# Second layer of a bidirectional recurrent trunk: gate groups in four parts between the projection units, the square root of 1 - a a in another form, and the convolution's first tap on ScalarE

## The chip, the core and the metric

The kernel runs on one core of a Trainium2 chip. A core has a matrix engine (TensorE, PE in the rows; its weight loads are a queue of their own, PEld), VectorE (DVE), ScalarE (ACT), GpSimd (POOL) and SyncE (SP), which issues the DMAs. Each engine works through its own instructions in order and waits for the others on semaphores. The metric is the device time of one launch in microseconds; a comparison of this kernel tells a change of about 1% from no change.

## What is computed

The reference is one step of a two-layer trunk with width D = 1024 on T = 1152 tokens, 128 of context and 1024 latents. Layer 0 (a gated recurrence and an attention) isn't touched by the change. Layer 1, cut to what matters:

```python
def odd_mixer(h, w_in, w_out, conv_w, conv_b, gate_w, gate_b, lam, s0):
    xb, g = jnp.split(h @ w_in, 2, axis=-1)
    xc = centred_dwconv(xb, conv_w, conv_b).astype(jnp.float32)   # width 4
    ...
    for d in range(2):
        gates = jnp.einsum('bthi,ghij->gbthj', xblk, gate_w[d].astype(jnp.float32)).reshape(2, B, T, W_C)
        gates = gates + gate_b[d].astype(jnp.float32)[:, None, None, :]
        r = jax.nn.sigmoid(gates[0])
        i = jax.nn.sigmoid(gates[1])
        log_a = -RG_C * r * jax.nn.softplus(-lam[d].astype(jnp.float32))
        a = jnp.exp(log_a)
        u = jnp.sqrt(-jnp.expm1(2.0 * log_a)) * (i * xc)
        ...
        hs, h_fin = linear_recurrence(a, u, s0[:, d].astype(jnp.float32))
    y = ((outs[0] + outs[1]) * jax.nn.silu(g.astype(jnp.float32))).astype(h.dtype)
    return y @ w_out, jnp.stack(finals, axis=1)
```

The gate matrices are block diagonal: 8 blocks of 128 features, two directions d, two gates each.

## The kernel before, in words

Features lie on the partitions, tokens along the free axis, in 3 chunks of 384. Every product is made of three matmuls, since operands are split into a high and a low part (names ending in h and l). In layer 1 the input projection is a sequence of 48 units (a block of 128 features times a chunk), of 24 matmuls each (L316 to L318). Its order, `ORD1`, is the x branch of blocks 0 to 3, then the g branch of block 0, x of block 4, g of block 1 and so on, and g of blocks 4 to 7 at the end. An x unit is copied by ScalarE to `xp`; a g unit is turned by ScalarE and VectorE (L1161) into `sg`.

Around the units stands the work of each block j, at positions in the sequence that the tables `PF`, `PC`, `PK`, `PS` and `PY` give (block by block; the change leaves them as they are):

- `conv` at `PC`: four taps on VectorE (L1049 makes `xc` from `xp`, L1051 three more), then the split into `xch` and `xcl` for the matmuls.
- `gates` at `PF`: for each direction and chunk, a group of 3 matmuls for each of two gates, 12 groups a block. The groups of the r gate go to the PSUM tag a (`ps_a`), those of the i gate to the tag b (`ps_b`), two banks each. ScalarE takes each group out by a tanh (`gr` from `ps_a`; `yT` or `gi` from `ps_b`).
- `rg_exp`, right behind the gates: on ScalarE `rt` = tanh of the decay's exponent and `gr` = a by exp; then `ra` = a a (GpSimd at L1102 for d = 0, ScalarE for d = 1) and on VectorE (1 + a a) times `rt` (L1103).
- `rg_sqrt` at `PS`: two square roots on ScalarE, which need a table of their own: an ACT_TABLE_LOAD stands ahead of them, and one behind them for the next tanh.
- `rg_scan` at `PK`: the input of the recurrence (L1116 on VectorE, L1118 on GpSimd, which multiplies by `rt`), seven scans on VectorE (L1127) and the sum of both directions (L1132). `y_fin` (L1167) multiplies by `sg`.

A unit's product lies in a PSUM bank of the tag mm (three banks) or, every fourth unit, of the tag o (one bank). A unit can't start before the bank that it takes over has been read, by the copy to `xp` or by L1161.

The order on each engine isn't written out: a scheduler takes the operations in the order in which the program writes them as their priority, and lays down one queue for each engine. What the tables say is therefore where an operation is written, and the queues follow from that and from the scheduler's own view of when operands are there. The output projection behind the units (L984 to L986) accumulates over 8 blocks k; its first two tiles take the terms of blocks 6 and 7 last.

Of the kernel before, what the change touches and what calls it, by code (L numbers as in the profile page):

```python
# [1 line left out]

# [16 lines left out]
CW = 384  # L19
# [3 lines left out]
# columns of the packed small parameters (feature on the partition)  # L23
# [10 lines left out]
def trunk_kernel(ctx: ExitStack, tc: tile.TileContext, x, wm0, wm, bmr, wfe, wv, woe, wfo, woo, rgw, sm, st0,  # L34
# [34 lines left out]
    def act(out, in_, func, **kw):  # L69
        """An activation; those that need a table of their own stay between its load and the next one."""  # L70
# [12 lines left out]
    # ------------------------------------------------------------------ constants  # L83
# [39 lines left out]
    # decay floors: the first entry of the softmax over the two logits  # L123
# [12 lines left out]
    # log1p(exp(-|lam|)) + max(-lam, 0), as a series in z = e / (2 + e) <= 1/3  # L136
# [17 lines left out]
    V.tensor_scalar(rgc, sp_t[3], 4.0, None, OP.mult)  # L154
# [3 lines left out]
    # ------------------------------------------------------------------ weight stream  # L158
# [43 lines left out]
    # ------------------------------------------------------------------ adaLN rows  # L202
# [86 lines left out]
    def to_hT2(l, c, ks, xn, tag):  # L289
        """Two blocks at once, each engine's steps together."""  # L290
# [18 lines left out]
    # ------------------------------------------------------------------ units of the projections  # L309
# [10 lines left out]
    def unit_f(i, c, tag=None):  # L320
        """Features of one block of 128 on the partition, one chunk of tokens."""
# [7 lines left out]
    def unit_v(i, t):  # L329
        """Tokens on the partition, 256 features."""  # L330
# [29 lines left out]
    def gate_evac(key, o, twice=False):  # L360
        """o sigmoid(o); twice that by way of sigmoid(o) = (1 + tanh(o / 2)) / 2."""
# [22 lines left out]
    # ------------------------------------------------------------------ start  # L384
# [81 lines left out]
    # ------------------------------------------------------------------ layer 0, gated recurrence  # L466
# [17 lines left out]
    def ew1(h, d):  # L484
        """Log decays, their running sums in chunks of 64 and the sums' distances from each chunk's middle."""
# [877 lines left out]
```

## Time and profile before

| | us |
|---|---|
| median of three runs | 1321.14 (1316.18 to 1326.65) |
| span of the profiled execution | 1308.3 |
| time of the profiled execution itself | not recorded apart from its span |
| median less span | 12.8 |
| granted TensorE clock over the span (1 is full) | 0.972 |
| TensorE busy over the span | 1210.3 (93%) |
| stretch of layer 1 that the rows look at, from the span's start | 925 to 1210 |

The span is the time between the first and the last instruction of one execution on the chip. In the rows, L-numbers are lines of the kernel before, `out<-in` the names of the tiles, an amount in brackets behind `<-` the idle time of the engine ahead of the instruction and what ended it. "x24" is a number of instructions. Where a group's row has two numbers behind the bar, the first is its whole time and the second the mean of one in ns.

### The profile page before, as it was taken

How to read it: one execution, taken by the hardware profiler on the slowest of the kernel's cores; microseconds unless marked ns; L12 is line 12 of the kernel's file. 1: busy time of each engine (PE TensorE's matmuls, PEld its weight loads, DVE VectorE, ACT ScalarE, POOL GpSimd, SP SyncE). 2: the span in 40 equal slices, each digit the busy share in tenths (PEclk: the TensorE clock that was granted, in tenths of full speed). 3: DMA queues.
4: the chain of work that ended last, by engine and by line, in shares of the span. 5: the costliest groups of instructions: out<-in, count | busy, mean ns of one | idle time of the engine just before them, and what ended most of it. 6: DMA issues, size and time to landing. Idle time of an engine off the chain costs nothing.

```text
span 1308.3 us, 19176 instructions
## 1 busy us (share of the span) xinstructions
PE 1210.3 (93%) x7536; PEld 1076.2 (82%) x7536; DVE 692.2 (53%) x1422; ACT 540.4 (41%) x1065; POOL 380.4 (29%) x271
## 2 busy tenths in 40 slices
PE   4999999999999966999989999999989898988998
PEld 3889998999998964779966667888989798987886
DVE  5547128316365100000058897555568978799844
ACT  3435134334253201111136675323376676777311
POOL 0143023321414101111150420025445663645000
PEclk8999999999999997999979999999999989999999
DMA  9401000111101236562240215324001101112432
GB/s 353 179 33 37 17 19 23 53 33 37 33 23 43 95 120 208 173 209 75 65 158 13 95 66 177 113 81 145 17 25 41 41 25 41 41 33 81 145 129 81
DMA packets 41909, 110.45 MB, mean 84 GB/s; under 512 B 4180, under 2 KB 14804, under 8 KB 41820
## 3 DMA queue, kind: packets, MB, share of 16 engines
q1 hardware_dynamic: 41820, 109.24, 24.4%
q8 instruction: 59, 0.97, 0.3%
q14 instruction: 30, 0.25, 0.1%
HBM read 96.61 MB, written 12.61 MB: 83 GB/s over the span
## 4 chain that ended last, share of the span: by engine, by line
PE 36%; DVE 12%; ACT 6%; issue 4%; POOL 2%; DMA 1%; POOLq 0%; ACTq 0%; DVEq 0%; SPq 0%
PE ps_mm L316 5%; PE ps_mm L318 5%; PE ps_mm L317 5%; PE ps_mm L985 5%; PE ps_mm L984 4%; PE ps_mm L986 4%; DVE yT L1127 2%; DVE xc L1051 2%; DVE P L849 2%; ACT P L77 2%; ACT gr L77 1%; PE ps_a L221 1%; DMA bmrow<-in_bmr_dram 1%; DVE ps_mm L844 1%; ACT rt L77 1%
## 5 line engine op out<-in xcount | busy, mean ns | idle before, releaser
L316 PE MATMUL ps_mm<-hTh,wh 128*128 128x384 f32 x936 | 320.7, 347 | 9.9 <-ACT xp L77 4.8
L317 PE MATMUL ps_mm<-hTl,wh 128*128 128x384 f32 x936 | 319.8, 342 | 2.3 <-DVE hTl L307 1.7
L318 PE MATMUL ps_mm<-hTh,wl 128*128 128x384 f32 x936 | 319.4, 341 | 0.7 <-POOL wl L186 0.7
L186 POOL TENSOR_TENSOR wl<-wraw,wh 128x1024 fp32r<-128x1024 f32 x50 | 127.2, 2548 | 306.1 <-ACT wh L77 248.7
L316 PEld LDWEIGHTS ps_mm<-hTh,wh 128*128 128x128 f32 x936 | 177.8, 191 | 26.5 <-issue 6.5
L317 PEld LDWEIGHTS ps_mm<-hTl,wh 128*128 128x128 f32 x936 | 178.4, 191 | 4.8 <-DVE hTl L307 3.3
L318 PEld LDWEIGHTS ps_mm<-hTh,wl 128*128 128x128 f32 x936 | 178.2, 190 | 1.3 <-POOL wl L186 1.0
L985 PE MATMUL ps_mm<-wl,yh 128*128 128x512 f32 (+1 forms) x288 | 113.4, 394 | 4.6 <-DVE wl L186 4.5
L984 PE MATMUL ps_mm<-wh,yh 128*128 128x512 f32 (+1 forms) x288 | 112.7, 393 | 0.0
L986 PE MATMUL ps_mm<-wh,yl 128*128 128x512 f32 (+1 forms) x288 | 112.3, 390 | 0.0
L77 ACT ACTIVATE wh<-wraw 128x1024 fp32r<-128x1024 f32 x68 | 71.3, 1057 | 91.1 <-DMA wraw<-in_wfe_dram 67.3
L262 POOL TENSOR_TENSOR ss<-ss,nhalf 128x1 f32<-128x1 f32 x27 | 15.3, 565 | 242.9 <-DVE ss L261 185.8
L339 PE MATMUL ps_mm<-wh,hTh 128*128 128x256 f32 x288 | 82.6, 287 | 2.4 <-ACT va L77 2.4
L341 PE MATMUL ps_mm<-wh,hTl 128*128 128x256 f32 x288 | 81.2, 282 | 0.0
L340 PE MATMUL ps_mm<-wl,hTh 128*128 128x256 f32 x288 | 81.0, 281 | 0.0
L365 DVE SCALAR_TENSOR_TENSOR yT<-yT,ps_mm 128x384 f32<-128x384 f32 x10 | 5.5, 554 | 131.3 <-ACT yT L77 131.3
L77 ACT ACTIVATE res<-xt 128x512 f32<-128x512 f32 (+1 forms) x37 | 22.9, 619 | 123.3 <-DVE xt L994 115.5
L814 POOL TENSOR_TENSOR nbm<-mkt,bT 128x384 f32<-128x384 f32 x42 | 45.5, 1108 | 90.1 <-DVE nm L860 40.4
L985 PEld LDWEIGHTS ps_mm<-wl,yh 128*128 128x128 f32 x288 | 54.6, 189 | 19.0 <-DVE wl L186 7.7
L984 PEld LDWEIGHTS ps_mm<-wh,yh 128*128 128x128 f32 x288 | 54.5, 189 | 12.4 <-issue 0.3
L986 PEld LDWEIGHTS ps_mm<-wh,yl 128*128 128x128 f32 x288 | 54.4, 189 | 11.4
L1118 POOL TENSOR_TENSOR yT<-yT,rt 128x384 f32<-128x384 f32 x42 | 56.4, 1370 | 23.4 <-ACT rt L77 19.4
(260 smaller groups left out, 2477.3 us busy)
## 6 DMA issues: line engine op xcount, KB each, us to landing
wm<-in_wm_dram SPq DMA_DIRECT2D x48, 512.0 KB
wraw<-in_wfe_dram SPq DMA_DIRECT2D x28, 512.0 KB
xt<-in_x_dram SPq DMA_DIRECT2D x18, 512.0 KB
bT<-in_bias_dram SPq DMA_DIRECT2D x48, 192.0 KB
wraw<-in_wfo_dram SPq DMA_DIRECT2D x16, 512.0 KB
x_d<-xt SPq DMA_DIRECT2D x9, 512.0 KB
xt<-x_d SPq DMA_DIRECT2D x9, 512.0 KB
out_dram<-xt SPq DMA_DIRECT2D x18, 256.0 KB
```

The source lines that it names most:

```text
L77: i = A.activation(out, in_, func, **kw)
L186: (lo_eng or G).tensor_tensor(lo, r, hi.bitcast(F32), OP.subtract)
L316: PE.matmul(o, w1, hh, start=(k == 0), stop=False)
L317: PE.matmul(o, w1, hl, start=False, stop=False)
L318: PE.matmul(o, w2, hh, start=False, stop=(k == 7))
L339: PE.matmul(o, hh, w1, start=(k == 0), stop=False)
L340: PE.matmul(o, hh, w2, start=False, stop=False)
L341: PE.matmul(o, hl, w1, start=False, stop=(k == 7))
L984: PE.matmul(o[:, :q - p], yh[:, z], wh[:, p:q], start=(k == 0), stop=False)
L985: PE.matmul(o[:, :q - p], yh[:, z], wl[:, p:q], start=False, stop=False)
L986: PE.matmul(o[:, :q - p], yl[:, z], wh[:, p:q], start=False, stop=(k == 7))
L1118: G.tensor_tensor(us[c], us[c], r[:, c * CW:(c + 1) * CW], OP.mult)
```

## The change

Three edits, all in layer 1.

The first splits the gates. Before, `rg_front(j)` wrote all 12 groups of a block and both `rg_exp` at position `PF[j]`. Now `gates(j, part)` writes three groups at a time, at the positions `PF[j]` + 0, 1, 2 and 3 (no later than `PS[j]`), with a unit between; the groups alternate between `ps_a` and `ps_b`. `rg_exp(j, 0)` follows part 1, `rg_exp(j, 1)` part 3.

The second computes the square root of 1 - a a as (1 + a) times the square root of tanh(y / 2), with y the negative logarithm of a. The tanh's factor `rgc` is halved, `ra` and L1103 go, and after each square root VectorE multiplies by (1 + a) (line 1111 of the kernel after).

The third makes the convolution's first tap an activation (Identity with a scale and a bias for each partition) on ScalarE.

```diff
-    V.tensor_scalar(rgc, sp_t[3], 4.0, None, OP.mult)
+    V.tensor_scalar(rgc, sp_t[3], 2.0, None, OP.mult)
...
-        V.tensor_scalar(acc, xp[:, 0:1155], w[0], smc("convb", j), OP.mult, OP.add)
+        act(acc, xp[:, 0:1155], AF.Identity, scale=w[0], bias=smc("convb", j))
...
-    def gates(j, d):
+    GD = {}
+    GROUPS = [(d, c, q) for d in range(2) for c in range(3) for q in range(2)]
+
+    def gates(j, part):
...
+        for d, c, q in GROUPS[3 * part:3 * part + 3]:
...
+        if part == 1:
+            GD.pop((j, 0))
+            rg_exp(j, 0)
+        if part == 3:
+            GD.pop((j, 1))
             XS.pop(j)
             gw.pop(j)
+            rg_exp(j, 1)
...
         act(t, r, AF.Tanh, scale=rgc[:, ci], bias=rgc[:, ci])
         act(r, r, AF.Exp, scale=nrgc[:, ci], bias=nrgc[:, ci])
-        t2 = slab("ra")
-        if d:
-            act(t2, r, AF.Square)
-        else:
-            G.tensor_tensor(t2, r, r, OP.mult)
-        V.scalar_tensor_tensor(t, t2, 1.0, t, op0=OP.add, op1=OP.mult)
 
     def rg_sqrt(j, d):
         act(RT[j, d], RT[j, d], AF.Sqrt, scale=0.25)
+        V.scalar_tensor_tensor(RT[j, d], GR[j, d], 1.0, RT[j, d], op0=OP.add, op1=OP.mult)
...
-        for p, f in ((max(ends[j], PC[j]), conv_all), (PF[j], rg_front), (PS[j], rg_root), (max(PK[j], PS[j]), rg_back),
+        for p, f in ((max(ends[j], PC[j]), conv_all), *[(min(PF[j] + n, PS[j]), partial(gates, part=n)) for n in range(4)],
+                     (PS[j], rg_root), (max(PK[j], PS[j]), rg_back),
```

The numbers of instructions: TensorE's matmuls and the 26 table loads are the same; GpSimd loses 8 `ra`; ScalarE loses 8 squares and gains 8 first taps; VectorE loses 8 first taps, and 16 products with (1 + a a) become 16 with (1 + a).

Three places show how the queues move. The first is ScalarE around the first square roots of layer 1, those of block 0. Before, all six r gates of block 0 (`gr` from `ps_a`) and both exp stand there, then the square roots of `rt`; the five `yT` behind them are the i gates of the next block, whose r gates come later:

```order
L77 ACTIVATE gr<-ps_a,hgb 128x384 x4
L77 ACTIVATE rt<-gr,rgc 128x1152
L77 ACTIVATE gr<-ps_a,hgb 128x384 x2
L77 ACTIVATE gr<-gr,nrgc 128x1152
L77 ACTIVATE rt<-gr,rgc 128x1152
L77 ACTIVATE gr<-gr,nrgc 128x1152
L74 ACT_TABLE_LOAD
L77 ACTIVATE ra<-gr 128x1152
L77 ACTIVATE rt<-rt 128x1152
L77 ACTIVATE gw<-gwr 128x512
L77 ACTIVATE rt<-rt 128x1152
L74 ACT_TABLE_LOAD
```

The same place now, where the three `gr` are the second direction of block 0, and the `gr` and `yT` at the end belong to block 1:

```order
L78 ACTIVATE wh<-wraw 128x1024
L78 ACTIVATE gr<-ps_a,hgb 128x384 x3
L78 ACTIVATE rt<-gr,rgc 128x1152
L78 ACTIVATE gr<-gr,nrgc 128x1152
L75 ACT_TABLE_LOAD
L78 ACTIVATE rt<-rt 128x1152 x2
L75 ACT_TABLE_LOAD
L78 ACTIVATE gr<-ps_a,hgb 128x384
L78 ACTIVATE yT<-ps_b,hgb 128x384
```

What moved: the first direction's tanh and exp stand elsewhere, earlier, and behind the second table load r and i groups of block 1 take turns. On TensorE the last r group of block 0 now stands inside unit 16, followed there by block 1's first two r groups; the third one and five more groups stand at the end of unit 16, and unit 17 behind them.

The second place is VectorE around the g units of block 0 (`sg`). Before, the two products with (1 + a a) of L1103 are followed at once by the three `sg`, and by `y_fin`:

```order
L1127 SCALAR_TENSOR_TENSOR yT<-gr,yT 128x256
L1128 COPY rgfin<-yT 128x1
L1132 TENSOR_TENSOR yT<-yT 128x384 x3
L1103 SCALAR_TENSOR_TENSOR rt<-ra,rt 128x1152 x2
L1161 SCALAR_TENSOR_TENSOR sg<-sg,ps_mm 128x384 x2
L1161 SCALAR_TENSOR_TENSOR sg<-sg,ps_o 128x384
L1167 SCALAR_TENSOR_TENSOR yT<-yT,sg 128x384 x3
```

Now the rows run as follows; `L1111`, the product with (1 + a) of block 0 for both directions, stands five rows ahead of the first one shown (the scans are printed by the order as SCALAR_TENSOR_TENSOR with three operands):

```order
L1121 SCALAR_TENSOR_TENSOR yT<-yT,xc 128x128
L1121 SCALAR_TENSOR_TENSOR yT<-yT,xc 128x256
L1132 SCALAR_TENSOR_TENSOR yT<-gr,yT 128x384
L1121 SCALAR_TENSOR_TENSOR yT<-yT,xc 128x384
L1132 SCALAR_TENSOR_TENSOR yT<-gr,yT 128x384
L1132 SCALAR_TENSOR_TENSOR yT<-gr,smt,yT 128x384
L1121 SCALAR_TENSOR_TENSOR yT<-yT,xc 128x384
L1132 SCALAR_TENSOR_TENSOR yT<-gr,yT 128x384
L1133 COPY rgfin<-yT 128x1
L1137 TENSOR_TENSOR yT<-yT 128x384
L1166 SCALAR_TENSOR_TENSOR sg<-sg,ps_mm 128x384
```

What moved: the first `sg` (L1166 after the change) now stands behind the two products and block 0's scans (L1132 after the change), where it stood right behind the products.

The third place is VectorE at the convolution of block 4. Before, its taps and the scans of another block take turns:

```order
L1049 TENSOR_SCALAR xc<-xp,smt 128x1155
L1127 SCALAR_TENSOR_TENSOR yT<-gr,yT 128x128
L1051 SCALAR_TENSOR_TENSOR xc<-xp,smt,xc 128x1155
L1127 SCALAR_TENSOR_TENSOR yT<-gr,smt,yT 128x256
L1051 SCALAR_TENSOR_TENSOR xc<-xp,smt,xc 128x1155
L1127 SCALAR_TENSOR_TENSOR yT<-gr,yT 128x384
L1051 SCALAR_TENSOR_TENSOR xc<-xp,smt,xc 128x1155
L1127 SCALAR_TENSOR_TENSOR yT<-gr,yT 128x384
L1057 TENSOR_TENSOR xcl<-xc,xch 128x128
```

Now:

```order
L1172 SCALAR_TENSOR_TENSOR yT<-yT,sg 128x384
L1052 SCALAR_TENSOR_TENSOR xc<-xp,smt,xc 128x1155 x3
L1058 TENSOR_TENSOR xcl<-xc,xch 128x128
L1144 MEMSET xp 128x2
L1145 MEMSET xp 128x3
L1058 TENSOR_TENSOR xcl<-xc,xch 128x1024
```

What moved: the three taps that are left stand together, ahead of the scans. The convolutions of blocks 3 and 6 stand like this one; those of blocks 5 and 7 still take turns with scans.

## Rows read from the trace of the kernel before

**Rows 1.** The page of the profiled execution: busy time of each engine, share of the span.

```profile
PE 1210.3 (93%) x7536; PEld 1076.2 (82%) x7536; DVE 692.2 (53%) x1422; ACT 540.4 (41%) x1065; POOL 380.4 (29%) x271
```

**Rows 2.** Waits of TensorE, 925 to 1210 us: total us, times, longest.

```profile
PE ps_a L1080 <- ACT gr L77: 8.7, 3, 3.5
PE ps_b L1080 <- ACT yT L77: 6.1, 1, 6.1
PE ps_mm L316 <- ACT xp L77: 4.8, 1, 4.8
PE ps_mm L316 <- DVE sg L1161: 2.0, 1, 2.0
```

**Rows 3.** Timeline of TensorE: start, us, and the idle time before in brackets.

```profile
979.81 0.69 PE L316 MATMUL ps_mm<-hTh,wh 128*128 128x384 f32 x1 [4.84 <-ACT xp L77]
...
1048.68 0.69 PE L1080 MATMUL ps_b<-xch,gw 128*128 128x384 f32 x1 [6.11 <-ACT yT L77]
...
1083.87 0.44 PE L1080 MATMUL ps_a<-xch,gw 128*128 128x384 f32 x1 [3.28 <-ACT gr L77]
```

**Rows 4.** Stretches: busy us (instructions) PE, PEld, DVE, ACT, POOL; granted clock; DMA share, GB/s.

```profile
930.00:970.00 40.00, 39.95 (x225) 38.61 (x224) 23.86 (x29) 26.08 (x38) 12.50 (x10) 1.00 0.10 34
970.00:1010.00 40.00, 35.16 (x181) 33.80 (x181) 35.95 (x42) 25.55 (x38) 24.34 (x14) 0.91 0.11 34
1010.00:1050.00 40.00, 32.00 (x176) 30.79 (x175) 38.00 (x50) 23.55 (x35) 21.49 (x11) 0.97 0.10 33
1050.00:1090.00 40.00, 36.72 (x189) 35.71 (x188) 31.53 (x47) 30.34 (x42) 20.55 (x11) 0.90 0.09 29
...
1130.00:1170.00 40.00, 36.47 (x199) 36.04 (x199) 29.60 (x42) 26.52 (x36) 19.63 (x12) 0.96 0.11 34
```

**Rows 5.** Groups by form, 925 to 1210 us: busy us, mean ns, idle time before.

```profile
L77 ACT ACTIVATE gr<-ps_a,hgb 128x384 f32<-128x384 f32 x48 | 26.5, 582 | 13.4 <-PE ps_a L1082 13.2
L1102 POOL TENSOR_TENSOR ra<-gr 128x1152 f32<-128x1152 f32 x8 | 25.7, 3214 | 53.4 <-ACT gr L77 35.5 <-DVE gi L1116 13.4 <-issue 4.5
L1103 DVE SCALAR_TENSOR_TENSOR rt<-ra,rt 128x1152 f32<-128x1152 f32 x16 | 23.7, 1493 | 26.4 <-POOL ra L1102 24.3 <-ACT ra L77 2.1
...
L77 ACT ACTIVATE gr<-gr,nrgc 128x1152 f32<-128x1152 f32 x16 | 21.6, 1351 | 0.3
L77 ACT ACTIVATE rt<-gr,rgc 128x1152 f32<-128x1152 f32 x16 | 21.5, 1343 | 0.0
L74 ACT ACT_TABLE_LOAD x15 | 19.2, 1283 | 0.3
...
L77 ACT ACTIVATE rt<-rt 128x1152 f32<-128x1152 f32 x16 | 18.2, 1159 | 0.1
...
L1049 DVE TENSOR_SCALAR xc<-xp,smt 128x1155 f32<-128x1155 f32 x8 | 13.4, 1673 | 6.8 <-PE ps_o L317 3.4 <-ACT xp L77 3.4
```

**Rows 6.** Waits of the other engines, 925 to 1210 us.

```profile
ACT xch L77 <- DVE xc L1051: 39.0, 7, 11.3
...
DVE rt L1103 <- POOL ra L1102: 24.3, 6, 9.3
```

**Rows 7.** Timeline of VectorE: two convolutions.

```profile
934.70 0.88 DVE L1049 TENSOR_SCALAR xc<-xp,smt 128x1155 f32<-128x1155 f32 x1 [3.38 <-ACT xp L77]
935.62 4.33 DVE L1051 SCALAR_TENSOR_TENSOR xc<-xp,smt,xc 128x1155 f32<-128x1155 f32 x3
...
1095.64 2.96 DVE L1049 TENSOR_SCALAR xc<-xp,smt 128x1155 f32<-128x1155 f32 x1
```

**Rows 8.** Timeline of VectorE: first and last scan of a block.

```profile
1111.66 1.21 DVE L1127 TENSOR_TENSOR_SCAN yT<-gr,yT 128x128 f32<-128x128 f32 x1 [1.19 <-POOL yT L1118]
...
1119.51 1.02 DVE L1127 TENSOR_TENSOR_SCAN yT<-gr,yT 128x384 f32<-128x384 f32 x1
```

**Rows 9.** GpSimd's first product of block 7.

```profile
1201.47 3.10 POOL L1118 TENSOR_TENSOR yT<-yT,rt 128x384 f32<-128x384 f32 x3 [10.80 <-ACT rt L77]
```

**Rows 10.** VectorE: block 7's last split.

```profile
1218.26 2.89 DVE L967 TENSOR_TENSOR yl<-yT,yh 128x384 fp32r<-128x384 f32 x6
```

More of the change, by code (lines that the diff above doesn't have):

```diff
@@ L1 @@
 from contextlib import ExitStack
+from functools import partial
 import concourse.bass as bass
@@ L1057, in conv @@
             V.tensor_tensor(lo[:, a:b], xc_of(j, a, b), hi[:, a:b].bitcast(F32), OP.subtract)
-    def gates(j, d):
+    GD = {}
+    GROUPS = [(d, c, q) for d in range(2) for c in range(3) for q in range(2)]
+    def gates(j, part):
         hi, lo = XS[j]
         wh, wl = gw[j]
-        GR[j, d] = slab("gr")
-        dst = [mini("yT") for c in range(3)] if d == 0 or j < 6 else None
-        if d == 0:
-            for c in range(3):
-                yT[j, c] = dst[c]
-        else:
-            if dst is None:
-                gi = slab("gi")
-                dst = [gi[:, c * CW:(c + 1) * CW] for c in range(3)]
-            GI[j] = dst
-        for c in range(3):
-            z = slice(c * CW, (c + 1) * CW)
-            for q in range(2):
-                g = 2 * d + q
-                ps = psum(("a", "b")[q])
-                o = ps[:, :CW]
-                n = slice(g * 128, (g + 1) * 128)
-                PE.matmul(o, wh[:, n], hi[:, z], start=True, stop=False)
-                PE.matmul(o, wh[:, n], lo[:, z], start=False, stop=False)
-                PE.matmul(o, wl[:, n], hi[:, z], start=False, stop=True)
-                i = (d * 2 + q) * 8 + j
-                act(GR[j, d][:, z] if q == 0 else dst[c], o, AF.Tanh, scale=0.5, bias=hgb[:, i:i + 1])
-        if d == 1:
@@ new lines, in gates @@
+        for d, c, q in GROUPS[3 * part:3 * part + 3]:
+            if (j, d) not in GR:
+                GR[j, d] = slab("gr")
+                dst = [mini("yT") for _ in range(3)] if d == 0 or j < 6 else None
+                if d == 0:
+                    for cc in range(3):
+                        yT[j, cc] = dst[cc]
+                else:
+                    if dst is None:
+                        gi = slab("gi")
+                        dst = [gi[:, cc * CW:(cc + 1) * CW] for cc in range(3)]
+                    GI[j] = dst
+                GD[j, d] = dst
+            z = slice(c * CW, (c + 1) * CW)
+            g = 2 * d + q
+            ps = psum(("a", "b")[q])
+            o = ps[:, :CW]
+            n = slice(g * 128, (g + 1) * 128)
+            PE.matmul(o, wh[:, n], hi[:, z], start=True, stop=False)
+            PE.matmul(o, wh[:, n], lo[:, z], start=False, stop=False)
+            PE.matmul(o, wl[:, n], hi[:, z], start=False, stop=True)
+            i = (d * 2 + q) * 8 + j
+            act(GR[j, d][:, z] if q == 0 else GD[j, d][c], o, AF.Tanh, scale=0.5, bias=hgb[:, i:i + 1])
@@ L1168, in y_fin @@
         SG.pop(j)
-    def rg_front(j):
-        gates(j, 0)
-        gates(j, 1)
-        for d in range(2):
-            rg_exp(j, d)
     def rg_root(j):
```

1 line of the change is left out of this document (removed).

## The prediction

> **What bounds the kernel now.** I read the page first: TensorE is busy for 93% of the span, VectorE for 53% and ScalarE for 41% [rows 1]. No change to the other engines can therefore give more than the time in which TensorE waits or runs slowly in layer 1. The next view is its waits there. They are four kinds [rows 2]: 8.7 us for r gates' banks in three places, 6.1 us for an i gate's bank, 4.8 us for a copy to `xp`, 2.0 us for `sg`; 21.6 us together. The timeline shows the three longest, 4.84, 6.11 and 3.28 us [rows 3]; the fourth is the 3.5 us that rows 2 give as the longest of the `ps_a` waits.
>
> What such a wait costs beside itself is read from the stretches of 40 us [rows 4]. The stretch ahead of the first wait has a granted clock of 1.00; those with the waits have 0.91, 0.97, 0.90 and 0.96. As shares of 40 us the losses are 3.6, 1.2, 4.0 and 1.6 us, 10.4 us in all: after the long waits TensorE runs for a while at the lower of its two levels (1.2 GHz instead of 2.4). So **the ceiling** is 21.6 + 10.4 = 32 us.
>
> What ends the waits is ScalarE's queue, and what holds ScalarE is seen in the waits of the others: `xch` waited 39.0 us in seven places for the last tap of `xc`, and `rt` on VectorE 24.3 us for GpSimd's `ra` [rows 6]. While ScalarE stands at `xch`, the tanh of the next gate group and the copies to `xp` stand behind it, and so do the banks that they would free.
>
> **The change, part by part.** A unit takes 24 matmuls and a group 3; in the undisturbed stretch 225 matmuls took 39.95 us [rows 4], 0.178 us each, so a unit takes 4.26 and a group 0.53 us.
>
> *What goes for certain.* The 24.3 us of VectorE's waits for `ra` [rows 6] and 25.7 us of GpSimd [rows 5] go; neither is on TensorE's path by itself, and what it is worth is what the copies and tanhs gain. Convolutions 3, 4 and 6 now stand free of scans on VectorE. The first tap took 0.88 us where GpSimd was quiet, 1.67 us as the mean of eight, and 2.96 us at the worst [rows 7, 5]. On ScalarE, 1155 columns of another activation take 1.34 to 1.35 us [rows 5], which I take for the new tap. I therefore write off the waits of 6.11, of 4.84 (moved, next paragraph) and the two of 1.9 and 2.0 us. The two of 3.28 and 3.5 us hang on the convolutions of blocks 5 and 7, which still take turns with scans; they lose the 1.67 us of the tap on VectorE each: 3.28 + 3.5 - 3.34 = 3.4 us stay. Were the tap's saving only 1.67 - 1.35 each, 6.1 us would stay.
>
> Of the tap's new place the Trainium skill, "ScalarE: Activation LUTs", section "Rules for kernel authors", says that a plain multiply or add belongs on VectorE and not on ScalarE. The undisturbed 0.88 us agrees with it and the mean of 1.67 us doesn't. By the rule the eight taps would lose 8 x (1.35 - 0.88) = 3.8 us if all stood on the path; the sum here would be that much higher.
>
> *Where a new wait stands: unit 16 and 17.* Let t = 0 be ScalarE's start on block 0's last r gate. Behind it, as the order has it, stand 0.58 (tanh) + 1.34 + 1.35 + 1.28 (table) + 2 x 1.16 (roots) + 1.28 (table) = 8.15 us, with the durations of rows 5. Only then comes the tanh of block 1's first r gate, another 0.58, which frees the bank for that block's third: 8.7 us. TensorE has meanwhile two groups and some 19 matmuls, 4.6 us. It waits 4.1 us. Then come this group, five more and unit 17. That unit needs a bank whose `sg` now stands on VectorE behind both products with (1 + a) and block 0's scans. The first root is done at 5.7; two products follow, taken at 1.44 us each, as a tap of the same size takes with GpSimd quiet (4.33 us for three [rows 7]; L1103, the same form beside GpSimd, took 1.49 [rows 5]), so 8.6; the seven scans of a block take from 1111.66 to 1120.5, 8.8 us [rows 8]; an estimate of 1.6 us for the four small operations between them and 0.5 each for a sum and for `sg` itself, all of a third of the products' columns or fewer: `sg` is done at 20.0. TensorE is ready for unit 17 at 8.7 + 6 x 0.53 = 11.9. It waits 8.1 us. Both together are 12.2 us, in the place of 4.84. The bounds: if ScalarE gets to the roots later than the gates need their banks, nothing of the 4.1 remains; if the scans have to wait for GpSimd's products (1.2 us before the first scan in rows 8), 3 us more.
>
> *A second such place.* Block 1's `sg` on the one bank of tag o stands in the same way behind two products, the scans, three sums and eight small operations. Between nothing and 8 us is lost there; I take the middle, 4 us. Of the g units further on, the order has `sg` behind scans as well, but these units are more than two units, 8.5 us, ahead of the one that needs the bank; I take nothing for them and price them as a rival.
>
> The waits become 12.2 + 4 + 3.4 = 19.6 us for 21.6: **-2.0**.
>
> *Clock.* The loss of 10.4 us came from four long waits. Of the new ones two are long (8.1 and 4); the stretch with the 4.84 us wait lost 3.6 us [rows 4], so two cost 7.2 at the most, and I take 3.4 for each as for a wait that starts inside its stretch: 6.8. **-3.6.**
>
> *The end.* Block 7's chain runs from the last r gate through roots, GpSimd's product, scans and splits to the last products of the first output tiles. Before, GpSimd's product had waited 10.80 us for the square root [rows 9], and the last splits start at 1218.26 [rows 10], where TensorE has come to these terms: no slack. The product with (1 + a) of the first direction, 1.44 us, now stands between. The last gate group of block 7 also stands behind unit 48, so that its tanh (0.58) is ahead of the table load: **+2.0** together. Without cover lost there it is 0; with an exp (1.35) also in the way it is 3.4.
>
> The sum against the profiled execution: 1308.3 - 2.0 - 3.6 + 2.0 = 1304.7. The profiled execution's own time isn't recorded; the median lies 12.8 us above its span, and I keep that: **about 1317.5 us**, a change of -0.3%. Whatever lies within 1% (1307.9 to 1334.4) would not be told from no change.
>
> **The rivals.**
>
> *Faster: the gates' waits vanish.* This is what splitting would do if ScalarE had no long block of work when the tanhs are due. All 21.6 us go but the 4.84 us that unit 17's neighbourhood keeps, of the clock's 10.4 us 3.4 stay, and the end costs 2: -16.8 - 7.0 + 2.0 = -21.8, so 1299.3 us. For it: convolutions 3, 4 and 6 stand clear, and 24.3 us of VectorE's idle time [rows 6] go. Against it: the roots and both tables still stand in one piece ahead of block 1's tanhs.
> A second reason for it is seen in the three taps of rows 7: 4.33 us, 1.44 each, where GpSimd is quiet; with GpSimd at `ra` the same work is dearer, as the first tap's 0.88 against 2.96 us shows. The Trainium skill, "GPSIMD Engine Reference", section "Key points", says that the two engines share ways into the SBUF, so that VectorE's instructions with two inputs there contend with GpSimd's. With GpSimd's 25.7 us of `ra` gone it speaks for this rival.
>
> *Slower: `sg` behind the scans costs at every g block.* Before, `sg` followed L1103 at once. Now it stands behind 2.9 us of products, 8.8 of scans and three sums of 0.5, 13.2 us. The next unit but two needs the bank after 8.5 us: 4.7 us of waiting, and 1.7 of clock, at three blocks more: 3 x 6.4 = 19 us, so 1317.5 + 19 = 1337 us. It decides when the roots end less than 8.5 us ahead of a g unit's own end; only where they end after it are the scans really in the way. For it: VectorE is busy for 38.0 of 40 us in the stretch from 1010 [rows 4]. Against it: 24.3 us of its waits and 13.4 us of first taps go, so that scans start earlier.
>
> *The splitting changes nothing.* ScalarE's queue is in order, and groups that were split on TensorE are read in the old rhythm. The waits then stay at about 21.6 us and only the roots' new form and the tap act, in both directions: about 1321 us. It lies so close to the forecast that I count it with it.
>
> **How the numbers follow.** The forecast with the last rival, 1310 to 1330 us, 0.44; the faster rival, 0.31; the slower one, 0.25. The forecast's own range comes from its bounds: -8 us if place one and two cost only half, +12 if the convolutions of blocks 5 and 7 keep 6.1, place two costs 8, the end 3.4 and the clock all of its 10.4. Over all cases the range is 1297 to 1340: from a little under the faster rival (the end without cost) to a little above the slower one. The chances follow: faster by over 1% 0.31, within 1% 0.44, slower by over 1% 0.25.
>
> **What would show it.** In the profile after: TensorE's waits in layer 1 at about 19 us, with `ps_a` waiting for ScalarE by some 4 us and a unit waiting for `sg` by some 8 us near the first roots; no wait of 6 us behind the convolution of block 4; `xch` waiting clearly less than 39 us; two stretches with a clock under 0.95 instead of four. The prediction is wrong on the fast side if the waits of `ps_a`, `ps_b` and `sg` sum to under 8 us, on the slow side if waits for `sg` are seen at four or more places, or if VectorE shows a busy share of over 95% in two stretches.

## The result, and the profile after

The changed kernel took 1362.89 us (median of four runs, 1351.6 to 1370.02), the kernel before 1322.85 us beside it. The ratio is 1.0313, with a 95% interval of 1.0271 to 1.0354: **slower by 3.1%, 40 us**. 1317.5 us were forecast.

The profiled execution of the changed kernel has a span of 1368.2 us, 60 us more than that of before. Part of this isn't the change's. The granted clock varies from execution to execution of one kernel, and with it the time, so that medians below are of all executions of a kernel and ratios leave its slow ones out. Layer 1's first unit began at 903.8 us in the execution of rows 1 to 10, here at 922.7, although the change doesn't touch what lies ahead; this execution was the longest of the four. So what follows compares the stretch of layer 1's units alone, from their first matmul to their last. The view of stretches gives busy time (instructions) of PE, PEld, DVE, ACT and POOL, then the granted clock, DMA share and GB/s. Of the kernel before:

```profile
903.80:1194.50 290.70, 268.00 (x1466) 261.09 (x1466) 229.57 (x300) 193.90 (x279) 155.64 (x87) 0.96 0.13 43
```

Of the changed kernel, the same stretch and then 40 us at a time:

```profile
922.70:1251.70 329.00, 283.40 (x1463) 275.39 (x1463) 218.56 (x295) 191.54 (x276) 133.59 (x79) 0.91 0.12 38
...
970.00:1010.00 40.00, 35.58 (x196) 34.39 (x195) 12.76 (x16) 24.14 (x36) 9.06 (x6) 0.97 0.09 27
1010.00:1050.00 40.00, 31.90 (x156) 31.39 (x155) 28.33 (x39) 24.13 (x35) 14.08 (x11) 0.81 0.07 20
1050.00:1090.00 40.00, 33.58 (x165) 32.62 (x165) 29.08 (x40) 23.18 (x33) 19.40 (x12) 0.87 0.12 36
1090.00:1130.00 40.00, 27.94 (x139) 26.66 (x138) 31.16 (x40) 22.31 (x31) 16.23 (x10) 0.88 0.09 31
...
1170.00:1210.00 40.00, 32.88 (x156) 31.92 (x157) 32.20 (x39) 24.13 (x33) 21.46 (x10) 0.86 0.10 33
1210.00:1250.00 40.00, 36.74 (x185) 35.80 (x185) 29.27 (x44) 25.24 (x38) 11.09 (x7) 0.88 0.17 53
```

The units take 329.0 us for 290.7, 38.3 more: nearly all of the 40. TensorE's idle time there grows from 290.7 - 268.0 = 22.7 to 329.0 - 283.4 = 45.6 us, by 22.9; its matmuls (three fewer, a gate group of block 7 that now stands behind the last unit) take 283.4 for 268.0, 15.4 more, at a granted clock of 0.91 for 0.96. In five stretches of 40 us it lies from 0.81 to 0.88 [rows 4 have nothing under 0.90]. VectorE, ScalarE and GpSimd are all busy for less time than before.

The waits of TensorE in the stretch (total, times, longest), which answer to [rows 2]:

```profile
PE ps_a L1085 <- ACT gr L78: 29.3, 9, 4.4
PE ps_mm L317 <- DVE sg L1166: 8.1, 1, 8.1
PE ps_b L1085 <- ACT yT L78: 7.2, 5, 2.6
```

Waits for the gates' banks went from four (8.7 + 6.1 = 14.8 us) to 14 (36.5 us). The other waits didn't go away either, they were exchanged: 4.8 us for a copy to `xp` and 2.0 for `sg` became one wait of 8.1 us for `sg`. The timeline shows the place that the prediction had walked through, and three waits further on:

```profile
1008.54 0.69 PE L1085 MATMUL ps_a<-xch,gw 128*128 128x384 f32 x1 [4.42 <-ACT gr L78]
...
1022.76 0.69 PE L317 MATMUL ps_mm<-hTh,wh 128*128 128x384 f32 x1 [8.10 <-DVE sg L1166]
...
1101.17 0.45 PE L1085 MATMUL ps_b<-xch,gw 128*128 128x384 f32 x1 [2.58 <-ACT yT L78]
...
1104.91 0.69 PE L1085 MATMUL ps_a<-xch,gw 128*128 128x384 f32 x1 [2.95 <-ACT gr L78]
...
1128.20 0.69 PE L1085 MATMUL ps_a<-xch,gw 128*128 128x384 f32 x1 [4.33 <-ACT gr L78]
```

4.42 and 8.10 us, where 4.1 and 8.1 were worked out. The last three rows are of the many that weren't. ScalarE's timeline ahead of them, with what it stood for in brackets:

```profile
1098.54 0.87 ACT L78 ACTIVATE sg<-ps_mm 128x384 f32<-128x384 f32 x2 [4.97 <-DVE yT L1132]
1099.30 1.35 ACT L78 ACTIVATE rt<-gr,rgc 128x1152 f32<-128x1152 f32 x1
1100.54 0.58 ACT L78 ACTIVATE yT<-ps_b,hgb 128x384 f32<-128x384 f32 x1
1101.00 1.35 ACT L78 ACTIVATE gr<-gr,nrgc 128x1152 f32<-128x1152 f32 x1
1102.24 0.58 ACT L78 ACTIVATE yT<-ps_b,hgb 128x384 f32<-128x384 f32 x1
1104.28 1.05 ACT L78 ACTIVATE gr<-ps_a,hgb 128x384 f32<-128x384 f32 x2 [1.46 <-DVE yT L1121]
...
1119.39 1.11 ACT L78 ACTIVATE yT<-ps_b,hgb 128x384 f32<-128x384 f32 x2 [1.73 <-PE ps_b L1087]
1126.42 1.26 ACT L78 ACTIVATE xch<-xc 128x128 fp32r<-128x128 f32 x2 [5.93 <-DVE xc L1052]
1127.59 1.03 ACT L78 ACTIVATE gr<-ps_a,hgb 128x384 f32<-128x384 f32 x2
```

For this kernel's ScalarE the reader is to see that each group's tanh (0.6 us) stands somewhere in a queue of things that take or wait much longer: here `sg`, which waited 4.97 us for VectorE, tanh and exp of the decay (1.35 us each), and `xch`, which waited 5.93 us for the convolution; in the first place the roots between two loads. Whatever stands ahead of the tanh of the group before last in the same tag holds TensorE.

Read in this way, the 36.5 us of the 14 waits divide as follows (where two things held ScalarE, the longer one is named): roots and table loads 8.2 us in three places, `xch` 7.3 in two, `sg` waiting for VectorE 4.9 in two, the weights' copy `wh`, which itself had waited for its input or its tile, 8.5 in three, and tanh and exp of the decay with what they had waited for 7.6 in four. No one of them holds the most.

### The profile page after: what moved, and what is told of

Read it like the earlier page. It is cut to its first block, busy times and chain, and to the rows that moved or that the text cites. A ratio compares the mean times of both kernels' runs of the same rounds, so it can differ in the third digit from the quotient of the medians.

```text
span 1368.2 us, 19142 instructions
## 1 busy us (share of the span) xinstructions
PE 1243.8 (91%) x7536; PEld 1106.5 (81%) x7536; DVE 674.7 (49%) x1414; ACT 540.6 (40%) x1065; POOL 357.8 (26%) x263
## 3 DMA queue, kind: packets, MB, share of 16 engines
q1 hardware_dynamic: 41820, 109.24, 23.8%
## 4 chain that ended last, share of the span: by engine, by line
PE 33%; DVE 11%; ACT 6%; POOL 5%; issue 5%; DMA 2%; POOLq 0%; ACTq 0%; SPq 0%; DVEq 0%
PE ps_mm L317 4%; PE ps_mm L985 4%; PE ps_mm L986 4%; PE ps_mm L987 4%; PE ps_mm L319 4%; PE ps_mm L318 4%; POOL yT L1123 2%; DVE yT L1132 2%; POOL wl L187 2%; DVE P L850 2%; DVE xc L1052 1%; ACT P L78 1%; DMA bmrow<-in_bmr_dram 1%; PE ps_a L222 1%; PE ps_a L875 1%
## 5 line engine op out<-in xcount | busy, mean ns | idle before, releaser
L317 PE MATMUL ps_mm<-hTh,wh 128*128 128x384 f32 x936 | 326.0, 352 | 11.2 <-DVE sg L1166 8.1
L318 PE MATMUL ps_mm<-hTl,wh 128*128 128x384 f32 x936 | 325.2, 348 | 2.3 <-DVE hTl L308 1.7
L319 PE MATMUL ps_mm<-hTh,wl 128*128 128x384 f32 x936 | 325.1, 347 | 0.6 <-POOL wl L187 0.6
L187 POOL TENSOR_TENSOR wl<-wraw,wh 128x1024 fp32r<-128x1024 f32 x50 | 131.0, 2622 | 352.5 <-ACT wh L78 257.8
L317 PEld LDWEIGHTS ps_mm<-hTh,wh 128*128 128x128 f32 x936 | 181.8, 195 | 27.6 <-DVE sg L1166 8.6
L318 PEld LDWEIGHTS ps_mm<-hTl,wh 128*128 128x128 f32 x936 | 182.9, 195 | 4.6 <-DVE hTl L308 3.1
L319 PEld LDWEIGHTS ps_mm<-hTh,wl 128*128 128x128 f32 x936 | 182.4, 195 | 1.3 <-POOL wl L187 0.9
L1123 POOL TENSOR_TENSOR yT<-yT,rt 128x384 f32<-128x384 f32 x42 | 59.3, 1444 | 74.3 <-DVE rt L1111 74.3
L78 ACT ACTIVATE res<-xt 128x512 f32<-128x512 f32 (+1 forms) x37 | 22.9, 619 | 123.9 <-DVE xt L995 116.0
```

The lines of the kernel that those rows point to most:

```text
L78: i = A.activation(out, in_, func, **kw)
L187: (lo_eng or G).tensor_tensor(lo, r, hi.bitcast(F32), OP.subtract)
L317: PE.matmul(o, w1, hh, start=(k == 0), stop=False)
L318: PE.matmul(o, w1, hl, start=False, stop=False)
L319: PE.matmul(o, w2, hh, start=False, stop=(k == 7))
L1123: G.tensor_tensor(us[c], us[c], r[:, c * CW:(c + 1) * CW], OP.mult)
```

## The experiments

Every run was timed in three rounds beside the kernel before; a ratio is to that, with its 95% interval. "Units" is the stretch from layer 1's first matmul of a unit to its last in the run's profile, as above (290.7 before, 329.0 after). One profile each makes it good to some us only, so no verdict rests on a difference under 10.

### Which of the three edits

The split alone (the kernel before, with the changed `gates` and positions, and L1103 and the first tap as they were):

```diff
+            *[(min(PF[j] + n, PS[j]), partial(gates, part=n)) for n in range(4)],
```

> The kernel before with the gates in four parts and nothing else of the change. Theory A (the split itself: gate groups now stand all along TensorE's queue with two banks for each tag, and TensorE comes to them while ScalarE is in a table load, an exp or a wait): this run holds most of the loss, 25 to 45 us slower than before, with waits of ps_a and ps_b for ScalarE of 30 us or more in layer 1. Rival B (the product with 1 + a between the root and GpSimd's product makes the scans late, their tiles come free late, and ScalarE stands for them): this run is within 10 us of before. Rival C (only the three together are slow): within 10 us too.

Measured: 1368.49 us, 1.0382 (1.0329 to 1.0434); units 333.1. The gates' banks were waited for 36.0 us, in 11 places. The split alone holds all of the loss.

The root alone:

```diff
-        V.scalar_tensor_tensor(t, t2, 1.0, t, op0=OP.add, op1=OP.mult)
...
+        V.scalar_tensor_tensor(RT[j, d], GR[j, d], 1.0, RT[j, d], op0=OP.add, op1=OP.mult)
```

> The kernel before with only the new form of the square root: factor 2, no a a, no product with 1 + a a, a product with 1 + a behind each root. Theory A: within 8 us of before, GpSimd's waits for that product near 20 to 30 us. Rival B: 20 us slower or more, with GpSimd's product waiting 70 us for VectorE. Rival C: within 10 us.

Measured: 1334.55 us, 1.0117 (1.0048 to 1.0186); units 294.9. Rival B falls: the extra step behind the root costs 10 us in the medians, not 20 or more, and GpSimd's product waits 28.8 us for it, not 70. It is a little more than the 8 us that theory A allowed.

The tap alone:

```diff
+        act(acc, xp[:, 0:1155], AF.Identity, scale=w[0], bias=smc("convb", j))
```

> The kernel before with only the convolution's first tap on ScalarE. Theories A and B: within 6 us of before, since 8 x 1.35 us come to ScalarE and 8 x 1.67 us leave VectorE. If the tap behind ScalarE's queue delays the convolutions (VectorE's second tap waited 23.5 us for ScalarE in the changed kernel): 8 to 15 us slower.

Measured: 1335.13 us, 1.0140 (1.0059 to 1.0221); units 298.6. The medians are 10.9 us apart, more than the 6 that theory A allowed and within the 8 to 15 of a tap that delays the convolutions; it costs less than the split.

Root and tap, without the split (the changed kernel with `gates` and `rg_front` of before):

> The changed kernel without the split: the new root and the first tap on ScalarE, the gates as before. Theory A: within 10 us of before, that is 30 us or more faster than the changed kernel. Rival B: close to the changed kernel, 20 us or more above before. Rival C: between, 10 to 20 us above before.

Measured: 1320.83 us, 1.0005 (0.9965 to 1.0045); units 289.4. The two that each cost about 1% alone cost nothing together. In the stretch of units ScalarE is busy for 186.3 us with the root alone, 202.8 with the tap alone and 195.9 with both (193.9 before): the one relieves it where the other loads it. That this is the reason isn't shown. Theory A holds for the split, B and C fall.

### What of the split

The parts together:

```diff
-*[(min(PF[j] + n, PS[j]), partial(gates, part=n)) for n in range(4)]
+*[(PF[j], partial(gates, part=n)) for n in range(4)]
```

> The changed kernel with all four parts of a block written at the one position where the whole block's gates stood before (no unit between parts). Theory A1 (the units between the parts are the cause: groups are spread along TensorE's in-order queue, and each meets ScalarE at some other long work): back to within 10 us of before, waits of ps_a and ps_b together under 20 us. Rival D (the order inside a block is the cause: the first exp now stands between the parts): still 25 us or more above before.

Measured: 1328.06 us, 1.0033 (0.9994 to 1.0071). Its stretch of units:

```profile
927.70:1216.90 289.20, 269.60 (x1466) 259.97 (x1464) 219.88 (x299) 196.50 (x281) 133.22 (x79) 0.97 0.15 46
```

and its waits for gates there:

```profile
PE ps_a L1085 <- ACT gr L78: 14.0, 7, 5.2
PE ps_b L1085 <- ACT yT L78: 2.0, 3, 1.4
PE ps_b L1085 <- ACT gi L78: 2.0, 1, 2.0
```

18.0 us of gate waits for 36.5, a clock of 0.97 for 0.91, and 40 us less. It is the units between the parts that cost, not the cutting into parts and not the exp between them. Two more runs bear on it. Both exps behind the last part:

```diff
         if part == 1:
             GD.pop((j, 0))
-            rg_exp(j, 0)
...
+            rg_exp(j, 0)
             rg_exp(j, 1)
```

> The changed kernel with both directions' tanh and exp behind the last part instead of one behind part 1. Rival D (the 2.7 us of ScalarE between the parts hold the banks): 12 us or more faster than the changed kernel. Theory A1 and rival L: within 10 us of it.

Measured: 1357.76 us, 1.0280 (1.0219 to 1.0341); units 319.6: 5 us of the 40, as theory A1 had it. Two positions, one unit apart:

```diff
+*[(min(PF[j] + n // 2, PS[j]), partial(gates, part=n)) for n in range(4)]
```

> The changed kernel with the four parts at two positions one unit apart instead of four positions. Theory A1 (the stretch of the sequence over which groups are spread sets how often one meets a stretch in which ScalarE stands or is busy): between the parts together (1328) and the changed kernel (1363), about 1335 to 1350. If the mere cutting by units were the cause, whatever the distance: 1355 or more. If one unit between is free: 1328 within 8.

Measured: 1331.73 us, 1.0108 (1.0065 to 1.0151); units 300.6. That is less than the 1335 to 1350 of theory A1; by the expectation's numbers it is the case in which one unit between is free. The ratio is 0.75% above that of the parts together (2.8% for the whole spread), the units are 11 us longer (40): a third of the distance costs about a quarter.

The four parts two units earlier:

```diff
+*[(min(PF[j] - 2 + n, PS[j]), partial(gates, part=n)) for n in range(4)]
```

> The changed kernel with the four parts two units earlier (positions -2, -1, 0 and +1 instead of 0 to +3). Rival L (the spread makes a block's gates end 3 units later, so roots, scans and the tiles' release are late): 20 us or more faster than the changed kernel. Theory A1: within 12 us of the changed kernel, with ps_a and ps_b waits of 25 us or more.

Measured: 1373.86 us, 1.0456 (1.0347 to 1.0564); units 335.3. Rival L (everything behind the gates is late) falls. Among the waits of ScalarE in this run are two long ones of `rt`:

```profile
ACT rt L78 <- PE ps_mm L318: 10.4, 1, 10.4
ACT rt L78 <- PE ps_mm L319: 10.1, 1, 10.1
```

Two operations on `rt` wait 10 us each, by the trace for matmuls of units. Why early parts don't help isn't shown by this. The order on ScalarE around the roots is tested next.

### Loads or order

The kernel adds an order by hand: a table load stands behind every tanh and exp that is written ahead of it, and every one that is written behind it stands behind it. So each block's roots are a fence in ScalarE's queue. Without loads and fence, in the changed kernel (the root is left out here and in the three runs below; a scaling by 0.25 takes its place):

```diff
-        act(RT[j, d], RT[j, d], AF.Sqrt, scale=0.25)
+        act(RT[j, d], RT[j, d], AF.Identity, scale=0.25)
```

> The changed kernel with the square root left out (a scaling takes its place, so that the recurrence's input isn't what it should be) and with it the two table loads of each block, 2.6 us of ScalarE a block. Theory A2 (as the prediction had it, groups stand behind roots and tables): the three or more ps_a waits behind a table load go, 15 us or more faster than the changed kernel. Theory A1 and rival L: 5 to 12 us faster, since only 3 of 14 waits over 0.8 us end behind a table load in the changed kernel's timeline.

Measured: 1336.31 us, 1.0079 (1.0028 to 1.0130), 27 us less than the changed kernel; units 305.9. Its waits for gates in them are 33.9 us in 12 places, hardly fewer than the changed kernel's 36.5 in 14:

```profile
PE ps_a L1085 <- ACT gr L78: 29.4, 10, 7.7
PE ps_b L1085 <- ACT yT L78: 3.4, 1, 3.4
...
PE ps_b L1085 <- ACT gi L78: 1.1, 1, 1.1
```

What went is the wait of 8.1 us for `sg`, and 12.5 us of TensorE's busy time (270.9 for 283.4, at a clock of 0.94 for 0.91). By the expectation this spoke for theory A2, the loads; but the edit takes away two things. The fence kept, only the loads gone (the scaling is listed as if it needed its own table):

```diff
+            if fake or chain.get("fake"):
+                chain.update(bar=chain["users"], load=None, set=SETS[func][0], users=[], fake=fake)
...
+        i = A.activation(out, in_, AF.Identity if fake else func, **kw)
         if func in SETS:
-            after(i.ins, [chain["load"]])
+            after(i.ins, [chain["load"]] if chain["load"] else chain["bar"])
```

> As the run without tables (a scaling in place of the root), but with the order kept that the loads enforced: on ScalarE all tanh and exp that are written ahead of a block's roots stand ahead of them, all that are written behind stand behind. The run without tables and without that order took 1336 us. If the 2.6 us of loading a block are what it saved (theory A2): 1336 within 10 us. If the enforced order is (gate groups written behind the roots can't be taken out ahead of them): 1352 or more, close to the changed kernel's 1363.

Measured: 1360.6 us, 1.0326 (1.0232 to 1.0421); units 330.0: as slow as the changed kernel. Theory A2 falls. The loading costs nothing that can be told within the intervals; with the fence the time is back that the run before had saved. The counterparts with the parts together, first without fence (`PF[j]` for all parts, and the scaling):

> The parts together (1328 us) with a scaling in place of the root, so without the loads and the order that they enforce. It is the counterpart of the spread kernel without loads and order (layer 1's units took 305.7 us there, 328.8 in the changed kernel, 289.1 with the parts together). If the loads and the order cost a burst of gates as much as a spread block (23 us): the units take about 266 us. If they cost mainly spread groups: 280 or more, so that the spread without order costs 25 us or less of its 40.

Measured: 1351.64 us, 1.0202 (1.0108 to 1.0296); units 312.0: slower than with loads and fence (1328). By its number the second case of the expectation holds (units of 280 or more), but neither had foreseen a loss. The waits of that run have 47.7 us of ScalarE at `xch`, for 25.4 with loads and fence; why the scheduler's queues are worse there isn't shown. Then with the fence and without loads:

> The parts together, a scaling in place of the root, nothing loaded, the order that the loads enforce kept. If that order is what spread groups stop at and bursts don't: units about 280 to 292 us (289 with the loads, 312 without order), that is some 40 us less than the same kernel spread (329.8). If the missing loads make the scheduler lay out worse whatever the order: about 312.

Measured: 1330.61 us, 1.0037 (0.9994 to 1.0080); units 297, a little over the 280 to 292 of the first case. The stretches of units, first the spread kernel without fence, then with it, then the same two with the parts together (four kernels, one row of the same view each):

```profile
930.70:1236.60 305.90, 270.91 (x1466) 264.42 (x1465) 217.99 (x304) 177.74 (x267) 122.79 (x82) 0.94 0.14 43
```

```profile
908.40:1238.40 330.00, 278.04 (x1463) 270.21 (x1462) 219.86 (x295) 173.91 (x262) 130.62 (x79) 0.91 0.12 38
```

```profile
917.60:1229.60 312.00, 274.40 (x1465) 266.64 (x1464) 226.23 (x295) 176.29 (x263) 125.19 (x84) 0.93 0.13 40
```

```profile
912.20:1209.20 297.00, 270.79 (x1464) 262.36 (x1463) 216.17 (x299) 178.31 (x267) 130.74 (x79) 0.96 0.14 45
```

The gate waits of the last one are 22.3 us:

```profile
PE ps_a L1087 <- ACT gr L80: 18.3, 6, 5.1
PE ps_b L1087 <- ACT yT L80: 3.7, 1, 3.7
...
PE ps_b L1087 <- ACT gi L80: 0.3, 1, 0.3
```

| units, us (ratio to before) | parts together | parts spread | spread costs |
|---|---|---|---|
| fence and loads | 289 (1.0033) | 329 (1.0313) | +40 (+2.8%) |
| fence, no loads | 297 (1.0037) | 330 (1.0326) | +33 (+2.9%) |
| neither | 312 (1.0202) | 306 (1.0079) | -6 (-1.2%) |

The spread costs 33 to 40 us where the fence stands, with loads or without, and nothing where it doesn't. Half of the turn from +40 to -6 us is that the parts together lose 23 us without the fence, so the row says that the fence decides which of the two is better, and not that spread groups wait less without it.

### Distance, number, banks, and ScalarE's standing

Is it the distance between a block's last part and the next block's first, where the roots have to fit? The parts of blocks 0, 1, 3 and 4 alone spread (short distances), then those of 2, 5, 6 and 7 alone:

```diff
+*[(min(PF[j] + n * (j in (0, 1, 3, 4)), PS[j]), partial(gates, part=n)) for n in range(4)]
```

> The changed kernel with only blocks 0, 1, 3 and 4 spread over their positions; blocks 2, 5, 6 and 7 have their parts together. For these four the tables leave 1 or 2 units (4.3 or 8.5 us) between the last part and the next block's first, while ScalarE has some 9.3 us of tanh, exp, loads and roots to do there in a fixed order. Theory G (that distance is what costs): most of the 35 us between the parts together (1328) and the changed kernel (1363), 1346 or more. Theory N (every spread block costs the same): half, 1338 to 1348. If distances are no cause at all: below 1338.

```diff
+*[(min(PF[j] + n * (j in (2, 5, 6, 7)), PS[j]), partial(gates, part=n)) for n in range(4)]
```

> The changed kernel with only blocks 2, 5, 6 and 7 spread, whose last part has 3 or 4 units to the next block's first (block 7 has none behind it). Theory G: within 8 us of the parts together, 1336 or less. Theory N: half of the loss, 1338 to 1348.

Measured: 1342.1 us, 1.0150 (1.0074 to 1.0227), and 1342.66 us, 1.0102 (1.0025 to 1.0180); units 313.0 and 304.6. The short distances alone hold about half of the loss and not most of it, so theory G falls in its plain form, and N fits: over the parts together the halves cost 1.2% and 0.7%, and in the units 23.8 and 15.4 us, 39.2 for the 39.8 of all eight. That short distances cost somewhat more isn't excluded.

Is it that ScalarE stands for the convolution? `xch` by VectorE, in the changed kernel:

```diff
-            act(hi[:, a:b], xc_of(j, a, b), AF.Copy)
+            V.tensor_copy(hi[:, a:b], xc_of(j, a, b))
```

> The changed kernel with the copy of the convolution's result to its high part (xch, 128 and 1024 columns) on VectorE instead of ScalarE, so that ScalarE never stands for the convolution's last tap (32 us in seven places). Theory A1: the gates' waits that ended behind an xch (4.3 and 3.0 us, with the clock some 5 more) go, 8 to 20 us faster than the changed kernel. If ScalarE stands for the next thing instead, or VectorE's 1.3 us more a block are on the path: within 6 us of it.

Measured: 1357.09 us, 1.0268 (1.0201 to 1.0335); units 321.0. The waits of 32 us at `xch` are gone, and gates are waited for as long as before:

```profile
PE ps_a L1085 <- ACT gr L78: 26.2, 9, 8.5
PE ps_b L1085 <- ACT yT L78: 10.6, 4, 7.4
```

Something else stands ahead of the tanh then. This part of theory A1 (remove one of ScalarE's waits and its gate waits go) falls: 5.8 us of the 8 to 20.

Is it the two banks a tag? Five banks in turn for the groups, three for the units:

```diff
-        ps = psum(tag or ("o" if i >= IFO and ucount[0] % 4 == 0 else "mm"))
+        ps = psum(tag or "mm")
...
-            ps = psum(("a", "b")[q])
+            gcount[0] += 1
+            ps = psum("o" if gcount[0] % 5 == 0 else ("a", "b")[gcount[0] % 5 % 2])
```

> The changed kernel with the bank of tag o given to the gates: five banks in turn for the groups instead of four, and three for the units instead of four. If two banks a tag are what makes TensorE stop at a spread group: gate waits fall by a quarter or more (36.5 us before), 8 us or more faster than the changed kernel. If ScalarE's standing is so long that one bank more is filled too, or the units lose what the gates gain: within 6 us of it or slower.

Measured: 1376.01 us, 1.0379 (1.0291 to 1.0467); units 333.6: no faster than the changed kernel. Gate waits stay (18.9 + 9.2 + 7.5 = 35.6 us, though in 7 places for 14), and the units' waits for `sg` grow to 20.7 us in four places. One bank more is no cure if the units give it; a run with one more for the gates and none less for the units isn't there.

### The copy on VectorE without the split

`xch` on VectorE in the kernel with root and tap but without the split:

> The kernel with the new root and the first tap on ScalarE but the gates as before (1321 us), with the copy to xch on VectorE. If ScalarE's standing at xch (20 us in five places there) still reaches TensorE: 5 to 12 us faster than before. If units and whole bursts of gates have the slack for it, as theory A1 says: within 5 us of before.

Measured: 1315.64 us, 0.9940 (0.9902 to 0.9978); units 281.7: 47 us faster than the changed kernel, and 0.6% faster than before, less than the 1% named at the start, though the interval leaves 1 out. It is the first case of the expectation (5 to 12 us faster), against what theory A1 had said. Its stretch of units:

```profile
916.40:1198.10 281.70, 266.79 (x1465) 257.20 (x1464) 229.63 (x309) 186.71 (x265) 138.58 (x79) 0.98 0.13 44
```

15 us of idle time for 22.7. The same copy alone, in the kernel before:

> The kernel before with only the copy to xch on VectorE. If ScalarE's 39 us of standing at xch are what the faster version got rid of: 5 to 12 us faster than before. If it needs the room that the new root and the tap make on VectorE: within 5 us of before or slower.

Measured: 1329.59 us, 1.0042 (1.0007 to 1.0078); units 294.1, VectorE busy for 240.7 us in them for 229.6. It doesn't pay there. With root and tap VectorE is busy for 229.6 us with the copy, as long as before without it, so the room that the other two edits make is the likely reason; no run shows it apart.

## Why the prediction was wrong

**The ceiling and the reading of before** stand: the loss lies in layer 1's units, and it is waits and clock, as there.

**Place one** was right in mechanism: 4.42 and 8.10 us for 4.1 and 8.1. That the second number fits so well is luck. Counted from the same t = 0 (999.35), `sg` let unit 17 start at 23.4 us and not at 20.0, with scans that stood between GpSimd's products and other small operations; and TensorE had come there at 15.3 and not at 11.9, since its six groups ran at the lower level, a matmul every 0.32 us. (Two groups and 19 matmuls are 4.4 us by the prediction's own figures, not 4.6, which is of no weight.) The second place (4 us for block 1's `sg` on the bank of tag o) didn't come.

**The step that failed** is the one behind it: having priced one place where a gate group stands behind roots on ScalarE, the prediction wrote off the waits of 6.11 and 1.9 us and kept 3.4 for the other blocks, because it took the convolutions alone for what holds ScalarE there, and those of blocks 3, 4 and 6 now stand free of scans. Gate waits came at 14 places, 36.5 us for the 7.5 that the sum had (4.1 and 3.4). What held the groups of blocks 1 to 7 was the convolution in two places only (7.3 us); the others were roots and loads, `sg`, `wh`, and tanh and exp of the decay. Before, the twelve groups of a block came to ScalarE in one burst (four waits, 14.8 us); spread, some group of a block is next on TensorE during most of the sequence, and each meets what stands on ScalarE at that time.

The runs show the parts of this: the spread is the cause (329 us of units, 289 with nothing else changed than the positions), and neither taking away the loads, nor the standing at `xch`, nor a fifth bank for the groups cures it by itself. That the order around the roots decides is shown for the time (306 us of units without it, 330 with it and no loads), but not by way of the gate waits, which are 33.9 us without it; and the run with the parts together got worse without it. That interplay stays open.

**The clock** was forecast at -3.6 us and came at +15.4, some 40% of the loss in the units. The timeline has nine spells in which TensorE's matmuls of 384 columns take 0.52 us and not 0.34; before it has four. Each of the nine stands behind a wait: one behind the 4.42 and 8.10 us of place one (the row of 40 us with 0.81), five at once behind 2.95 to 4.33 us, three some 1 us behind 2.32, 2.80 and 3.10. The prediction had counted on two such places. The sum of the waits doesn't give the size, however: with both exps last the gate waits are 36.9 us and with `xch` on VectorE 36.8, as here, and TensorE is busy for 271.9 and 272.7 us there for 283.4. Why isn't shown.

**The end** was forecast at +2.0; from the last unit to the last matmul it is 108.8 us in the kernel without the split and 110.0 in the changed one, 107.2 before: +2.8.

**The tap and the root.** Of the eight taps on ScalarE (1.35 us each, as taken) the prediction's reserve was 3.8 us; alone they cost 1.4% (0.6 to 2.2), 10.9 us in the medians, and with the root nothing. The Trainium skill, "ScalarE: Activation LUTs", section "Rules for kernel authors", would have such an operation on VectorE. The tap alone agrees, the pair doesn't. The same section says to group by table set, and prices a switch at about 2.7 us. The trace has 1.28 us a load, with the operations ahead and behind at once beside it (an exp ends at 1003.07, the load runs from 1003.08 to 1004.36, the roots start at 1004.38), so that a switch is the load alone there, less than the page has. The runs show a price of another kind: the order that groups strictly goes with a cost of the spread of 33 to 40 us, and without it the spread costs nothing.

The three taps left on VectorE became faster, 1776 ns before, and after

```profile
L1052 DVE SCALAR_TENSOR_TENSOR xc<-xp,smt,xc 128x1155 f32<-128x1155 f32 x24 | 37.5, 1564 | 23.7 <-ACT xc L78 23.5
```

24 x 0.21 = 5 us less work on VectorE, and 23.5 us of new waiting for the tap on ScalarE in the same row. But `ra` wasn't what had made them dear, as the prediction read it: no `ra` stands beside a tap in the trace of before, and at its 2.96 us GpSimd was at `wl`. With `ra` kept the taps take 1552 ns (split alone) and 1568 (tap alone). What most of the dear ones stand beside is GpSimd's product for the recurrence:

```profile
972.27 4.48 POOL L1118 TENSOR_TENSOR yT<-yT,rt 128x384 f32<-128x384 f32 x3
972.79 2.11 DVE L1051 SCALAR_TENSOR_TENSOR xc<-xp,smt,xc 128x1155 f32<-128x1155 f32 x1
```

2.11 us for 1.44 with GpSimd quiet [rows 7]. The sharing that the Trainium skill describes in "GPSIMD Engine Reference", "Key points", agrees with this, not with the part given to `ra`. The faster rival, which leaned on it, needed ScalarE to have no long block of work when a tanh is due, and that is what it had.

**The slower rival** had the right side and 16 of the 40 us (1337, with 1340 as the upper end of the range), by another mechanism: `sg` behind the scans was waited for once, not at three more blocks. With 0.25 it had too little; its condition should have been put more widely, as any second thing in ScalarE's or VectorE's queue that a spread group meets.

**The base.** The 12.8 us between the span and the median were taken as lying around the span. Executions of the kernel before for which both are known have 1314.08 beside 1311.9, 2.2 us. The other 10.6 us were that the profiled execution of before was shorter than the median one. It didn't move the forecast, since the change was put on the median.

## What to carry to other kernels

Spreading small pieces of work along an in-order engine makes every one of them a place where that engine can stop; before counting the gain at one place, walk through all pieces against the queue of the engine that empties their buffers, and against any order that is enforced there. A stop can be paid twice: here most waits of 2.3 us and more were followed by a spell at the lower clock. And two edits that load and relieve the same engine are to be judged together: each of them alone cost about 1% here, and both cost nothing.

## What the runs showed of the hardware

The table loads of 1.28 us (15 in rows 5) left no mark on the time, within the 1% of the intervals, where the order around them was kept (ratios of 1.0326 without and 1.0313 with them; 330.0 and 329.0 us of units). A VectorE tap with three operands takes 2.1 us beside GpSimd's product of two SBUF tiles and 1.4 us alone.

Thirteen executions of the kernel before, beside the run with the split alone, had spans from 1311.9 us at a granted clock of 0.968 to 1337.9 us at 0.951. A single profile of this kernel therefore can't carry a small difference of the whole span, and the part of the trace that a change can't touch (here everything ahead of the units, 903.8 to 930.7 us in these runs) tells how much of a difference isn't its own.
